# A hybrid decoder layer: a ninth column block on TensorE, the first norm on turned rows, sample dots in three parts

## The chip, the core and the metric

One core of a Trainium2 chip runs the whole layer as one program. The metric is device time in microseconds (us), from the start to the end of one execution; runs of one kernel are summed up by their median. Where the profile is used, its times belong to one profiled execution. PE is TensorE, PEld its weight loads, DVE VectorE, ACT ScalarE, POOL GpSimd, SP the engine that issues most DMAs.

## The reference

256 prompt tokens and 32 sample tokens (8 sequences of 4) of width 2048 pass one layer: a mixer (RWKV-7 heads beside sparse attention heads), an output projection, a norm, an expert mixer and a second norm. Cut to the part that the change touches:

```python
def layer_norm(x, g, b):
    mu = x.mean(-1, keepdims=True)
    var = jnp.mean(jnp.square(x - mu), -1, keepdims=True)
    return (x - mu) * lax.rsqrt(var + LN_EPS) * g + b

def peer_ffn(x, wq, subkeys, u_tab, v_tab):          # x: (tokens, 2048)
    q = (x @ wq).reshape(n, 8, 2, 128)               # 8 heads, two halves of a key
    s = jnp.einsum('nhcd,hckd->nhck', q, subkeys)    # 128 sub-keys for each half
    hv, hix = lax.top_k(s, 16)
    cand = (hv[:, :, 0, :, None] + hv[:, :, 1, None, :]).reshape(n, 8, 256)
    cand_e = (hix[:, :, 0, :, None] * 128 + hix[:, :, 1, None, :]).reshape(n, 8, 256)
    tv, tpos = lax.top_k(cand, 16)
    expert = jnp.take_along_axis(cand_e, tpos, axis=-1)      # 16 of 16384 experts a head
    gate = jax.nn.softmax(tv, axis=-1)
    h = gelu(einsum('cd,chkd->chk', x, u_tab[expert]))       # 128 dots of 2048 a token
    return einsum('chk,chkd->cd', gate * h, v_tab[expert])   # 128 rows added a token

x = layer_norm(ALPHA * x + concat(y_r, y_n) @ w_out, ln1_g, ln1_b)
x = layer_norm(ALPHA * x + peer_ffn(x, ...), ln2_g, ln2_b)
```

## The kernel before

The prompt's 256 tokens are two tiles of 128, t = 0 and 1, in the partitions. Work is written as Python generators that are woven together. A scheduler then orders the instructions of each engine by a simulated time and by priorities; `tc.issue_after` and `tc.keep_in_program_order` (called `pin`) tie some of them down. Each engine runs its instructions strictly in that order. Tiles live in pools that are stacked from the left or the right end of the on-chip memory; a pool that is closed gives its space to later ones, and a tile in such space waits for the last user of what lay there.

The stages from the output product on:

1. **out**: `out_part(8, YN)` multiplies the second half of the mixer's result by `w_out`. Each fp32 factor is split into a rounded high part and a low part, and three matmuls give the product. Beside it runs `sample_chain`, the layer for the 32 sample tokens up to their first expert product: 128 partitions hold 32 tokens x 4 groups, and each of 32 choices needs two **sample dots** (line 1548): POOL gathers a 128x1024 half row of `peer_u` (`gather`, line 450) into a ring of five `cw` tiles, and DVE multiplies and sums it.
2. **ln1**: `layer_norm` for each prompt tile: statistics, then ACT normalises, DVE multiplies by the scale g, DVE and POOL in turn add the shift b. PE turns the finished rows into `XT` (2048 features in partitions), from which high and low parts `XHq`, `XLq` are made. The rows go to `X1D` in HBM, and the first 1024 columns come back as `X1a`.
3. **wq**: the query product, 16 column blocks c of 128 columns (`pj`, line 1806), copied by ACT to `QP`. For each head `scores` multiplies by the sub-keys (ACT copies the result to a ring `TB`), and `choose` takes the best 16 on DVE (lines 1359 to 1404), with POOL adding candidate indices and masking them (`L1406`). `settle`, one head later, reduces the masked indices (line 1412) and writes them, doubled, to `GI` (line 1413), the gathers' index table.
4. **peer**: a prompt token needs 128 dots of 2048 columns. For the upper 1024 columns PE computes them for *all* 16384 experts: `dense(i1)`, 128 steps of 128 experts, loads a turned block `ur` of the table `peer_u_t` and multiplies its eight column blocks by the tokens: two blocks in plain fp32 (line 1841), six split into high and low parts (ACT casts `uh`, DVE subtracts `ul`, 18 matmuls, line 1848). For the lower 1024 columns the 256 **prompt dots** (2 tiles x 128 choices) are gathered rows again (line 1772, ring `rows` of five). Constants spread them: `NDW` a head in wq from the third head on (6 in all), `ND` plus an extra one every `8/NDN` dense steps (160 in all), and the rest in weigh.
5. **weigh**: 68 software-pipelined, pinned steps pick the dense scores of the chosen experts: step s builds one-hot tiles `oo` on DVE (line 1880), PE turns and multiplies them (lines 1884, 1892), DVE takes the products (`xj`, line 1903), ACT scales (`scaled`), PE puts the weights into a table `AW` (`put`, line 1922). The first 28 steps carry the remaining prompt dots, later ones the sample's v rows, summed into `fs`. Then the sample's second norm and its 16 stores follow (lines 1983 to 1990).
6. **V** and **fin**: 128 steps multiply the weights by the upper table `peer_v` (1536 columns) while DVE adds gathered rows for the other 512, then the last norm.

## Time and profile before

| what | us |
|---|---|
| runs shown | 2556.65, 2556.81, 2553.73 (median 2556.65) |
| profiled execution | 2551.85 |
| its span | 2549.9 |
| PE busy / DVE busy / POOL busy / ACT busy in the span | 2250.9 / 1901.8 / 1380.0 / 985.3 |
| last matmul of the output product starts | 1046.87 |
| first matmul of the query product | 1088.73 |
| first dense matmul | 1223.43 |
| first one-hot tile of weigh | 1662.19 |
| second table row of the V stage reaches PE | 1996.43 |

Times inside the execution count from the start of the span. A group of the profile names line, engine, operation and tiles, the shapes, the count, the busy time and the mean of one in ns, and then the idle time of that engine before such instructions, with what ended it. In the chain of waits each row is a piece of the path that ended last. A plain fp32 matmul of 128x256 stands in the records as two, a split one as one.

### The profile page before, as it was taken

How to read it: one execution, taken by the hardware profiler on the slowest of the kernel's cores; microseconds unless marked ns; L12 is line 12 of the kernel's file. 1: busy time of each engine (PE TensorE's matmuls, PEld its weight loads, DVE VectorE, ACT ScalarE, POOL GpSimd, SP SyncE). 2: the span in 40 equal slices, each digit the busy share in tenths (PEclk: the TensorE clock that was granted, in tenths of full speed). 3: DMA queues.
4: the chain of work that ended last, by engine and by line, in shares of the span. 5: the costliest groups of instructions: out<-in, count | busy, mean ns of one | idle time of the engine just before them, and what ended most of it. 6: DMA issues, size and time to landing. Idle time of an engine off the chain costs nothing.

```text
span 2549.9 us, 44379 instructions
## 1 busy us (share of the span) xinstructions
PE 2250.9 (88%) x16140; PEld 1870.8 (73%) x16140; DVE 1901.8 (75%) x4264; ACT 985.3 (39%) x1845; POOL 1380.0 (54%) x1393
## 2 busy tenths in 40 slices
...
GB/s 223 234 221 238 282 218 147 114 203 231 225 240 263 249 237 253 311 253 180 188 380 369 363 362 362 358 265 275 242 268 236 277 318 324 325 345 323 320 326 167
DMA packets 343227, 683.28 MB, mean 268 GB/s; under 512 B 82142, under 2 KB 200864, under 8 KB 341696
## 3 DMA queue, kind: packets, MB, share of 16 engines
...
## 4 chain that ended last, share of the span: by engine, by line
PE 59%; DVE 15%; DMA 12%; issue 6%; POOL 5%; ACT 1%; SPq 1%; DVEq 0%; POOLq 0%; ACTq 0%
PE pb L2040 20%; PE ph L1848 9%; PE pj L419 7%; DVE rows L1772 3%; DMA rows<-in_peer_u,gi 3%; PE ph L1841 2%; PE pa L1664 2%; PE pj L1806 2%; DMA co<-in_cache_cmp_kv,gidx 2%; PE p L1076 2%; DVE CA L473 1%; PE pa L1922 1%; PE ss L1492 1%; DMA big<-in_state_rwkv 1%; PE px L1892 1%
## 5 line engine op out<-in xcount | busy, mean ns | idle before, releaser
L450 POOL DMA_INDIRECT rows<-in_peer_u,gi x256 | 356.0, 1391 | 231.1 <-DVE rows L1772 181.0
L450 POOL DMA_INDIRECT rq<-in_peer_v,gi x256 | 375.3, 1466 | 172.3 <-DVE fP L2014 77.9
L1772 DVE SCALAR_TENSOR_TENSOR rows<-rows,x1a 128x1024 f32<-128x1024 f32 x256 | 309.6, 1234 | 14.8 <-DMA rows<-in_peer_u,gi 14.5
L419 PE MATMUL pj<-XH,wl 128*128 128x288 f32 (+1 forms) x752 | 231.5, 308 | 15.6 <-POOL wl L414 8.3
L1848 PE MATMUL ph<-XHd,uh 128*128 128x256 f32 x768 | 239.1, 311 | 4.1 <-ACT uh L1635 0.8
L419 PE MATMUL pj<-XH,wh 128*128 128x288 f32 (+1 forms) x752 | 229.1, 305 | 11.5 <-DVE ss L749 7.0
L1848 PE MATMUL ph<-XHd,ul 128*128 128x256 f32 x768 | 225.2, 294 | 15.4 <-DVE ul L1636 13.1
L419 PE MATMUL pj<-XL,wh 128*128 128x288 f32 (+1 forms) x752 | 225.7, 300 | 0.0
L1848 PE MATMUL ph<-XLd,uh 128*128 128x256 f32 x768 | 218.1, 284 | 0.0
L2040 PE MATMUL pb<-vl,ah 128*128 128x512 f32 x768 | 217.8, 392 | 0.3 <-DVE vl L2034 0.3
L2040 PE MATMUL pb<-vh,al 128*128 128x512 f32 x768 | 216.5, 390 | 0.0
L2040 PE MATMUL pb<-vh,ah 128*128 128x512 f32 x768 | 199.1, 395 | 17.3 <-ACT vh L2033 17.3
L412 ACT CAST wh<-wraw 128x512 fp32r<-128x512 f32 (+1 forms) x188 | 114.5, 616 | 226.7 <-PE pj L419 168.3
L1636 DVE TENSOR_TENSOR ul<-ur,uh 128x384 fp32r<-128x384 f32 x256 | 135.2, 559 | 88.0 <-ACT uh L1635 87.1
L2014 DVE SCALAR_TENSOR_TENSOR fP<-rq,ge,fP 128x512 f32<-128x512 f32 x254 | 189.8, 747 | 2.4
L2040 PEld LDWEIGHTS pb<-vh,ah 128*128 128x128 f32 x768 | 146.3, 191 | 48.9 <-ACT vh L2033 18.5
L473 DVE SCALAR_TENSOR_TENSOR CA<-co,wbc,CA 128x256 f32<-128x256 f32 x248 | 135.9, 585 | 51.6 <-DMA co<-in_cache_cmp_kv,gidx 51.5
L1635 ACT CAST uh<-ur 128x384 fp32r<-128x384 f32 x256 | 125.5, 515 | 111.9 <-PE ph L1848 54.3
L2040 PEld LDWEIGHTS pb<-vl,ah 128*128 128x128 f32 x768 | 145.5, 190 | 31.2 <-DVE vl L2034 0.7
L1848 PEld LDWEIGHTS ph<-XHd,ul 128*128 128x128 f32 x768 | 147.6, 193 | 27.1 <-DVE ul L1636 26.3
L2040 PEld LDWEIGHTS pb<-vh,al 128*128 128x128 f32 x768 | 145.0, 189 | 30.4
L419 PEld LDWEIGHTS pj<-XH,wl 128*128 128x128 f32 (+1 forms) x752 | 143.7, 191 | 27.4 <-DVE wl L414 10.9
...
## 6 DMA issues: line engine op xcount, KB each, us to landing
ur<-in_peer_u_t SPq DMA_DIRECT2D x128, 512.0 KB
...
wraw<-in_w_in SPq DMA_DIRECT2D x64, 128.0 KB
...
```

What stands on the lines that cost most here:

```text
L412: sc.copy(wh[:, :, :n], w[:, :, :n])
L419: last[2] = pe.matmul(pb[:n, :nt], wi[:, k, :n], xi[(o + k) // 8][:, (o + k) % 8, :nt], start=(o + k == 0 and wi is wh and xi is xh), stop ...
L450: gp.indirect_dma_start(out=dst, out_offset=None, in_=rows_, in_offset=bass.IndirectOffsetOnAxis(ap=ix, axis=0))
L473: ve.scalar_tensor_tensor(d_, x_, w_, d_, op0=OP.mult, op1=OP.add)
L1076: pe.matmul(pb[hs[c], 64 * m:64 * m + 64], lhs(hs[c], m), rhs(hs[c], m), start=True, stop=True)
L1635: sc.copy(xh, pb)
L1636: return ve.tensor_tensor(xl, pb, xh.bitcast(F32), OP.subtract)
L1664: pe.matmul(acc[t], xi[:, e, P * t:P * t + P], wi[:, e, :], start=(k == e == n_ == 0), stop=(k == 6 and e == 1 and n_ == 2))
L1772: i_ = ve.scalar_tensor_tensor(r_, r_, 1.0, X1a[t], op0=OP.mult, op1=OP.mult, accum_out=h_)
L1848: mm = pe.matmul(ph[:, :NPR], wi[:, e, :], xi[:, NSP // 2 * q + e, :], start=False, stop=(q == 1 and e == NSP // 2 - 1 and wi is wl))
L2014: ve.scalar_tensor_tensor(fP[t], r_, w_, fP[t], op0=OP.mult, op1=OP.add)
L2040: pe.matmul(acc[3 * t + q], wi[:, P * t:P * t + P], xi[:, 512 * q:512 * q + 512], start=(k == 0 and wi is ah and xi is vh), stop=(k == P - ...
```

## The change

- **Nine column blocks on PE.** `NDB` = 9: `peer_u_t` has 1152 columns a row (576 KB a step), and the dense step has a third plain fp32 matmul. The prompt dots shrink to `UG` = 896 columns, gathered from a new contiguous table `peer_u_g`. Indices are no longer doubled. `NDN` goes from 2 to 4 (192 dots in peer), and wq carries prompt dots only in its last two rounds.
- **First norm.** Statistics are taken as each block of the output product is finished. One inverse root serves both tiles. DVE normalises without scale and shift, PE turns these rows, and ACT applies scale and shift as per-partition factors while it writes `XT`. The row form gets scale (DVE) and shift (POOL) afterwards, is stored from POOL's queue, and 896 columns are loaded back in round h = 2. `XHd` (ACT) and `XLd` (POOL) are made from `XT`.
- **Sample dots in three parts.** 28 in out (`NSD` = 14 choices), 12 in ln1 behind the normalising (`NLD` = 6), 24 in wq, four a round, with a ring `sr` of five tiles and a second copy `sx4` of the sample's x.
- **Smaller moves.** `settle`'s index write goes to POOL; the first query weights load earlier; the pools of out, wq, peer and V are laid out in another order (the V stage's tiles `v_`, `vh` lie first); the second norm's tiles for the sample lie in `x1a`'s space and load at step 46; the last `scaled` calls alternate between ACT and DVE; `out_part` gets a priority of 400 in the weaving.

The core of the diff:

```diff
+NSD = 14
+NLD = 6
...
-NDN = 2
+NDN = 4
...
-NSP = 6
+NDB = 9
+SPLIT = ((0, 3), (3, 6))
+NSP = SPLIT[-1][1]
+UG = 128 * (16 - NDB)
...
-        gp.tensor_copy(HF, HI)
-        gp.tensor_scalar(HF[:, 0], HF[:, 0], 128.0, None, op0=OP.mult)
+        k_ = 2.0 if t == 2 else 1.0
+        for c in range(2):
+            gp.tensor_scalar(HF[:, c], HI[:, c], k_ if c else k_ * P, 0.0, op0=OP.mult, op1=OP.add)
...
-        EF = pool([P, 16], "EF")
+        EF = pool([P, 16], "EF", bufs=2)
         ve.tensor_reduce(EF, hit, AX.X, OP.add)
-        ve.tensor_scalar(GI[t][:, 16 * h:16 * h + 16], EF, 2.0, None, op0=OP.mult)
+        gp.tensor_copy(GI[t][:, 16 * h:16 * h + 16], EF)
...
-        hd = cx([P, 2, 32], "hd")
...
-        for s_ in range(32):
+        yield from sample_dots(ring, x4, 0, NSD)
+
+    def sample_dots(ring, x4, n0, n1):
+
+        for s_ in range(n0, n1):
...
+    def sample_formed():
...
+                    ve.bn_stats(out=lst[:, t, cq, :], in_=x_)
...
+    np_.close()
...
-    weave((chain, 32), (out_part(8, YN), 16))
+    weave((chain, NSD), (out_part(8, YN), 16, 400))
...
-    XH, XL = (xq([P, NSP, NPR], nm, F32R) for nm in ("XHq", "XLq"))
+
+    kw_ = Pool("kw", "right")
+    wring = lambda: kw_([P, 8, P], "wraw", bufs=WB)
+    def query_load(c, o):
+
+        w = wring()
+        sy.dma_start(w, w_q[:, 128 * c:128 * c + 128].rearrange("(k p) c -> p k c", p=P)[:, o:o + 8])
+        return w
+
+    wq_ = {(0, o): query_load(0, o) for o in (0, 8)}
...
-        layer_norm(lp, lambda c0, n: x1c(t, c0, n),
-                   *(lambda c0, n, nm=nm: gb1[nm, c0 // 1024][:, c0 % 1024:c0 % 1024 + n] for nm in ("ln1_g", "ln1_b")))
-        for hf in range(2):
-            sy.dma_start(X1D[P * t:P * t + P, 1024 * hf:1024 * hf + 1024], X1[t][hf])
+        ve.bn_aggr(out=lmv[:, t, :], in_=lst[:, t].rearrange("p a b -> p (a b)"))
+    ve.tensor_scalar(lv, lmv[:, :, 1], 1e-5, None, op0=OP.add)
+    rsqrt(lp, lrr, lv, "ln")
+    ve.scalar_tensor_tensor(lv, lmv[:, :, 0], -1.0, lrr, op0=OP.mult, op1=OP.mult)
+    for t in range(2):
         for q in range(4):
+            x_ = x1c(t, 512 * q, 512)
+            normed = ve.tensor_scalar(x_, x_, lrr[:, t:t + 1], lv[:, t:t + 1], op0=OP.mult, op1=OP.add)
...
-            tk = slice(P * t, P * t + P)
-            n4 = min(4, NSP - 4 * (q % 2))
-            k4, p4 = slice(4 * (q % 2), 4 * (q % 2) + n4), pb.rearrange("p (k t) -> p k t", k=4)
-            sc.copy(XT[:, 4 * q:4 * q + 4, tk], p4)
-            if q > 1:
-                columns(p4[:, :n4], XH[:, k4, tk], XL[:, k4, tk])
+            for e in range(4):
+                k = 4 * q + e
+                sc.activation(XT[:, k, P * t:P * t + P], pb[:, 128 * e:128 * e + 128], AF.Identity,
+                              bias=prm("ln1_b", 16, k), scale=prm("ln1_g", 16, k))
+    sq_ = Pool("sq", "right")
+    sx4 = sq_([P, D], "sx4")
+    for g in range(4):
+        sy.dma_start(sx4[32 * g:32 * g + 32, :], X1D[NPR:NT, :])
+    late = sample_dots(lambda: sq_([P, 1024], "sr", bufs=5), sx4, NSD, 32)
+    with tc.issue_after(normed.ins):
+        for _ in take(late, NLD):
+            pass
+        for hf in range(2):
+            for t in range(2):
+                for nm, op_ in (("ln1_g", OP.mult), ("ln1_b", OP.add)):
+                    for q in range(2):
+                        x_, y_ = (t_[:, 512 * q:512 * q + 512] for t_ in (X1[t][hf], gb1[nm, hf]))
+                        (ve if op_ is OP.mult else gp).tensor_tensor(x_, x_, y_, op_)
+                gp.dma_start(X1D[P * t:P * t + P, 1024 * hf:1024 * hf + 1024], X1[t][hf])
     oe.close()
+    cx[0].close()
     lp.close()
-    cx[0].close()
-    np_.close()
...
-    TB = up([P, 4, NPR], "TB")
-    X1a = [up([P, 1024], f"x1a{t}") for t in range(2)]
-    for t in range(2):
-        sy.dma_start(X1a[t], X1D[P * t:P * t + P, :1024])
...
-    kc, dp, kq = (Pool(nm, "left") for nm in ("kc", "dp", "kq"))
+    up([P, 1024], "rows", bufs=NRW)
+    xa_ = up([P, 2 * UG], "x1a")
+    X1a = [xa_[:, UG * t:UG * t + UG] for t in range(2)]
+    TB = up([P, 4, NPR], "TB")
+    dp, kc, kq = (Pool(nm, "left") for nm in ("dp", "kc", "kq"))
+    dp([P, NDB, P], "ur", bufs=NUR)
     XHd, XLd = dp([P, NSP, NPR], "XHd", F32R), dp([P, NSP, NPR], "XLd", F32R)
-    Xfd = dp([P, 8 - NSP, NPR], "Xfd")
+    Xfd = dp([P, NDB - NSP, NPR], "Xfd")
...
-            rows_[i] = up([P, 1024], "rows", bufs=NRW)
-            gather(rows_[i], uh2, GI[t][:, s_:s_ + 1])
+            rows_[i] = up([P, 1024], "rows", bufs=NRW)[:, :UG]
+            gather(rows_[i], a["peer_u_g"], GI[t][:, s_:s_ + 1])
...
-                    w = kw_([P, 8, P], "wraw", bufs=WB)
-                    sy.dma_start(w, w_q[:, 128 * c:128 * c + 128].rearrange("(k p) c -> p k c", p=P)[:, o:o + 8])
+                    w = wq_.pop((c, o), None) or query_load(c, o)
...
-                sc.copy(QP[:, c, :], pb[:, :NPR])
+                last_ = sc.copy(QP[:, c, :], pb[:, :NPR])
...
+        if h == 2:
+            for t in range(2):
+                sy.dma_start(X1a[t], X1D[P * t:P * t + P, :UG])
...
-                if h > 2:
+                for _ in take(late, 2):
+                    pass
+                if h > 6:
...
+    with tc.issue_after(chosen.ins), tc.issue_after(last_.ins):
+        for _ in late:
+            pass
+        sample_formed()
+    sq_.close()
     kw_.close()
-    sc.copy(XHd, XH)
-    sc.copy(XLd, XL)
-    sc.copy(Xfd, XT[:, 8 + NSP:, :])
+    for q in range(NSP // 2):
+        k2, x_ = slice(2 * q, 2 * q + 2), XT[:, 16 - NDB + 2 * q:18 - NDB + 2 * q, :]
+        sc.copy(XHd[:, k2, :], x_)
+        gp.tensor_tensor(XLd[:, k2, :], x_, XHd[:, k2, :].bitcast(F32), OP.subtract)
+    sc.copy(Xfd, XT[:, 16 - NDB + NSP:, :])
...
-        w = dp([P, 8, P], "ur", bufs=NUR)
+        w = dp([P, NDB, P], "ur", bufs=NUR)
...
-        for e in range(NSP, 8):
+        for e in range(NSP, NDB):
             pe.matmul(ph[:, :NPR], w[:, e, :], Xfd[:, e - NSP, :], start=(e == NSP), stop=False)
-        for q in range(2):
-            wh, wl = (dp([P, NSP // 2, P], nm, F32R, bufs=3) for nm in ("uh", "ul"))
+        for e0, e1 in SPLIT:
+            wh, wl = (dp([P, e1 - e0, P], nm, F32R, bufs=3) for nm in ("uh", "ul"))
             with tc.high_priority(offset=120 + 45 * i1 if i1 < NPRI else 0):
-                lo_ = columns(w[:, NSP // 2 * q:NSP // 2 * q + NSP // 2, :], wh, wl)
-            for e in range(NSP // 2):
+                lo_ = columns(w[:, e0:e1, :], wh, wl)
+            for e in range(e0, e1):
                 for wi, xi in ((wh, XHd), (wh, XLd), (wl, XHd)):
-                    mm = pe.matmul(ph[:, :NPR], wi[:, e, :], xi[:, NSP // 2 * q + e, :],
-                                   start=False, stop=(q == 1 and e == NSP // 2 - 1 and wi is wl))
+                    mm = pe.matmul(ph[:, :NPR], wi[:, e - e0, :], xi[:, e, :],
+                                   start=False, stop=(e == NSP - 1 and wi is wl))
...
-            o_ = hot[u][:, 0, e, :]
-            pin(sc.activation(o_, o_, AF.Copy, scale=TB[:, 2, 4 * u + e:4 * u + e + 1]))
+            o_, g_ = hot[u][:, 0, e, :], TB[:, 2, 4 * u + e:4 * u + e + 1]
+            if u < 60 or e % 2:
+                pin(sc.activation(o_, o_, AF.Copy, scale=g_))
+            else:
+                pin(ve.tensor_scalar(o_, o_, g_, None, op0=OP.mult))
...
+        if s_ == 46:
+            bs_, gs_, x_ = (xa_[:, 512 * n:512 * n + 512] for n in range(3))
+            for q in range(4):
+                r_, c_ = slice(32 * q, 32 * q + 32), slice(512 * q, 512 * q + 512)
+                sy.dma_start(x_[r_, :], X1D[NPR:NT, c_])
+                for t_, nm in ((gs_, "ln2_g"), (bs_, "ln2_b")):
+                    sy.dma_start(t_[r_, :], bass.AP(tensor=a[nm].tensor, offset=a[nm].offset + 512 * q, ap=[[0, 32], [1, 512]]))
...
+    vp([P, FD], "v_", bufs=2)
+    vp([P, FD], "vh", F32R, bufs=2)
     fP = [vp([P, 512], f"fP{t}") for t in range(2)]
+    vp([P, 512], "rq", bufs=NRQ)
...
-        u_[:, 1024:].reshape(P, P, 8, P).transpose(0, 3, 2, 1)).reshape(P * P, 1024)
+        u_[:, UG:].reshape(P, P, NDB, P).transpose(0, 3, 2, 1)).reshape(P * P, P * NDB)
+    arrays["in_peer_u_g"] = np.ascontiguousarray(u_[:, :UG])
...
```

The order of the instructions at three places. First DVE, from the end of the output product to the first choice. Before, with `cw` the gathered row of a sample dot, `x_00` to `x_11` the halves of the two prompt tiles, `wraw` the rows of scale and shift, `ln_t` and `lnrr` the inverse root (a piece, the first tile's):

```order
L1548 SCALAR_TENSOR_TENSOR cw,hd<-cw,x_10488 128x1024
L1630 TENSOR_TENSOR x_00_9703<-x_00_9703,wraw 128x512
L1631 TENSOR_TENSOR x_00_9703<-x_00_9703,wraw 128x512
L243 SCALAR_TENSOR_TENSOR lnrr<-ln_t,lnrr 128x1
L1630 TENSOR_TENSOR x_01_9704<-x_01_9704,wraw 128x512 x2
L1548 SCALAR_TENSOR_TENSOR cw,hd<-cw,x_10488 128x1024 x2
L241 TENSOR_TENSOR ln_t<-lnrr 128x1
L1631 TENSOR_TENSOR x_01_9704<-x_01_9704,wraw 128x512
L1548 SCALAR_TENSOR_TENSOR cw,hd<-cw,x_10488 128x1024 x2
```

The same place now, from the end of the one inverse root on (`lnv` holds the shift of the normalising, `sr` the row of a sample dot, `shT` its result; `HV<-TB` is the first choice):

```order
L248 SCALAR_TENSOR_TENSOR lnrr<-ln_t,lnrr 128x2
L1733 SCALAR_TENSOR_TENSOR lnv<-lnmv,lnrr 128x2
L1737 TENSOR_SCALAR x_00_9713<-x_00_9713,lnrr,lnv 128x512 x2
L1737 TENSOR_SCALAR x_01_9714<-x_01_9714,lnrr,lnv 128x512 x2
L1737 TENSOR_SCALAR x_10_9715<-x_10_9715,lnrr,lnv 128x512 x2
L1737 TENSOR_SCALAR x_11_9716<-x_11_9716,lnrr,lnv 128x512 x2
L1558 SCALAR_TENSOR_TENSOR sr,shT<-sr,sx_12077 128x1024 x5
L1758 TENSOR_TENSOR x_00_9713<-x_00_9713,wraw 128x512 x2
L1758 TENSOR_TENSOR x_01_9714<-x_01_9714,wraw 128x512 x2
L1758 TENSOR_TENSOR x_10_9715<-x_10_9715,wraw 128x512 x2
L1758 TENSOR_TENSOR x_11_9716<-x_11_9716,wraw 128x512 x2
L1558 SCALAR_TENSOR_TENSOR sr,shT<-sr,sx_12077 128x1024 x7
```

The eight normalising operations stand alone behind the root; twelve sample dots and eight multiplies follow them and stand ahead of the first choice.

Second POOL at the same place, now: additions of the shift (L1758), stores of the rows to `x1d` (L1759) and the gathers of sample rows (L456).

```order
L456 DMA sr<-in_peer_u,ig 128x1024
L1758 TENSOR_TENSOR x_00_9713<-x_00_9713,wraw 128x512 x2
L1758 TENSOR_TENSOR x_01_9714<-x_01_9714,wraw 128x512 x2
L1758 TENSOR_TENSOR x_10_9715<-x_10_9715,wraw 128x512
L1759 DMA x1d<-x_00_9713 128x1024
L1758 TENSOR_TENSOR x_10_9715<-x_10_9715,wraw 128x512
L1758 TENSOR_TENSOR x_11_9716<-x_11_9716,wraw 128x512 x2
L456 DMA sr<-in_peer_u,gi_72 128x1024
L1759 DMA x1d<-x_01_9714 128x1024
L456 DMA sr<-in_peer_u,ig 128x1024
```

Ten gathers lie ahead of the additions; those of the eleventh and twelfth of the twelve dots lie behind them.

Third DVE at the seam between two rounds of the choice, before (`hit` is the last line of one head's choice, `L1404`; `gi` the index table):

```order
L1404 TENSOR_TENSOR rows<-CT_61,TF 128x864 x2
L1412 TENSOR_REDUCE EF<-rows 128x16
L1413 TENSOR_SCALAR gi_70<-EF 128x16
L1412 TENSOR_REDUCE EF<-rows 128x16
L1413 TENSOR_SCALAR gi_71<-EF 128x16
L1772 SCALAR_TENSOR_TENSOR rows,hd_12208<-rows,x1a_12204 128x1024
L1359 MAX HV<-TB 128x8 x2
```

And now:

```order
L1410 CAST TF<-TI 128x16 x2
L1411 TENSOR_TENSOR rows<-CT_61,TF 128x864 x2
L1419 TENSOR_REDUCE EF<-rows 128x16 x2
L1558 SCALAR_TENSOR_TENSOR sr,shT<-sr,sx_12077 128x1024 x4
L1365 MAX HV<-TB 128x8 x4
```

Four sample dots stand where the two index writes and one prompt dot stood.

45 lines of the change are left out of this document (14 added, 31 removed).

## The prediction

> **What bounds the kernel now.** The page gives a span of 2549.9 us (profiled execution 2551.85; the median of the runs shown, 2556.65, is 4.8 more). I read the busy time by stage first, because a share of the whole span mixes stages with different limits. Columns: stretch and length; busy time of PE, PEld, DVE, ACT, POOL with instructions; granted clock; DMA share; GB/s.
>
> ```profile
> 967.00:1047.00 80.00, 61.80 (x232) 47.04 (x232) 70.78 (x101) 21.05 (x29) 57.48 (x39) 0.81 0.87 313
> 1048.00:1117.00 69.00, 22.92 (x96) 18.75 (x96) 55.64 (x110) 13.39 (x22) 39.89 (x31) 0.63 0.85 295
> 1117.00:1234.00 117.00, 113.18 (x558) 100.19 (x559) 100.53 (x481) 18.46 (x42) 64.58 (x118) 0.98 0.53 158
> 1234.00:1350.00 116.00, 103.64 (x684) 94.34 (x684) 96.99 (x221) 47.73 (x97) 65.74 (x63) 0.96 0.90 341
> 1350.00:1660.00 310.00, 303.30 (x2086) 276.26 (x2085) 231.65 (x433) 144.27 (x284) 173.02 (x120) 1.00 0.97 361
> 1662.00:1842.00 180.00, 106.48 (x540) 98.27 (x541) 172.26 (x464) 63.65 (x168) 127.28 (x90) 0.68 0.80 265
> 1842.00:1980.00 138.00, 133.11 (x1005) 96.77 (x1003) 90.73 (x381) 91.51 (x252) 68.42 (x60) 0.97 0.71 240
> ```
>
> The stages are: output product, first norm, query product with the choice of experts, dense score product (two rows), the first 28 weigh steps, and the rest of them. The limit changes hands. In the norm PE works a third of the time and waits for DVE. From 1117 to 1660 PE is nearly full. From 1662 to 1842 DVE is (172.26 of 180), and PE waits for it. After 1842 PE is full again. The change takes dots from DVE in the weigh stage and gives PE a longer dense stage, so these two prices decide, with what the norm releases.
>
> Two waits of PE show how the norm holds up the query product. The timeline of PE, idle time and releaser in brackets:
>
> ```profile
> 1046.87 0.39 PE L1664 MATMUL pa<-wl,YH 128*128 128x512 f32 x1
> ...
> 1088.73 14.76 PE L1806 MATMUL pj<-XT,wraw 128*128 128x256 f32 x64
> ...
> 1117.47 8.91 PE L1806 MATMUL pj<-XT,wraw 128*128 128x256 f32 x32 [13.98 <-ACT QP L1807]
> ...
> 1233.66 0.58 PE L1848 MATMUL ph<-XHd,ul 128*128 128x256 f32 x1 [3.33 <-DVE ul L1636]
> ```
>
> Call the end of the output product T0 (1047.3). The query product starts at T0+41. It stops again for 14 us, until the last sample dot is done and QP's space is free. Dense steps flow from 1233.7, T0+186, with about two of the 128 done before.
>
> **Part 1: output product and norm.** Five of the 33 sample dots before T0 leave that stretch.
>
> ```profile
> L1548 DVE SCALAR_TENSOR_TENSOR cw<-cw,x 128x1024 f32<-128x1024 f32 x33 | 48.3, 1478 | 8.7 <-DMA cw<-in_peer_u,ig 6.7 <-DMA cw<-in_peer_u,gi 1.9
> ```
>
> Five times 1.478 is 7.4 us, if DVE alone sets T0. It is busy 70.78 of that stretch's 80 us and PE 61.80, so DVE sets most of it: the gain lies between 0 and 7.4, and I take 5, T0 = 1042. Behind T0 the old norm shows the paces of DVE and POOL, and the chain of work those of a gathered row:
>
> ```profile
> 1050.24 0.24 DVE L1625 BATCH_NORM_AGGREGATE lnmv<-lnst 128x2 f32<-128x24 f32 x1
> ...
> 1054.98 0.15 DVE L1434 SCALAR_TENSOR_TENSOR lnmv<-lnmv,lnrr 128x1 f32<-128x1 f32 x1
> ...
> 1056.52 0.68 DVE L1630 TENSOR_TENSOR x<-x,wraw 128x512 f32<-128x512 f32 x1
> ...
> L1631 POOL TENSOR_TENSOR x<-x,wraw 128x512 f32<-128x512 f32 x4 | 6.1, 1534 | 0.7 <-DVE x L1630 0.6
> ...
> 1066.78 7.83 DMA cw<-in_peer_u,gi
> ```
>
> One tile's chain of small operations takes 4.9 us with two dots inside, some 3 without, and now serves both tiles. Eight normalising operations follow, 0.68 us each at most (5.5). Transposes and ACT operations come block by block; the last trails by about 3 us. So the query product starts at T0+12, and the 14 us stall goes: QP's space no longer waits for all the sample dots.
>
> PE cannot use all of this, because DVE's order puts twelve sample dots and eight multiplies ahead of the first choice, and POOL's order puts eight additions ahead of the gathers for the last two of these dots. The additions cannot start before DVE has done five dots and the first multiplies, about T0+16; they take 8x1.5 = 12 us. Then come a gather (1.4), its landing (7.8 on the chain) and the dots: the first choice begins at T0+42. Bounds: T0+35, when the third product block gives head 0's scores (12+3x6.9) and rows come sooner, and T0+46.
>
> **Part 2: choosing rounds.** Each head costs one round on DVE. Timelines of DVE, then POOL, in one round:
>
> ```profile
> 1188.38 0.48 DVE L1359 MAX8 HV<-TB 128x8 f32<-128x128 f32 x2
> ...
> 1197.70 1.04 DVE L1412 TENSOR_REDUCE EF<-rows 128x16 f32<-128x864 f32 x1
> 1198.66 1.92 DVE L1772 SCALAR_TENSOR_TENSOR rows<-rows,x1a 128x1024 f32<-128x1024 f32 x1
> ...
> 1200.51 1.83 DVE L1413 TENSOR_SCALAR gi<-EF 128x16 int32<-128x16 f32 x1
> ...
> 1203.53 0.17 DVE L1413 TENSOR_SCALAR gi<-EF 128x16 int32<-128x16 f32 x1
> 1203.62 0.48 DVE L1359 MAX8 HV<-TB 128x8 f32<-128x128 f32 x2
> ...
> 1196.88 5.43 POOL L1406 TENSOR_TENSOR rows<-rows,CE 128x864 f32<-128x864 f32 x2
> ```
>
> A round is 15.24 us: 9.3 of choosing (1188.38 to 1197.70) and 5.9 behind it. Now two reductions (2.1) and four sample dots stand there, and the index writes are on POOL. At the dots' 1.145 us start to start (part 4) four cost 4.6: 16.0 us, if POOL's multiplies disturb nothing. They do: the dot takes 1.92, and the index write 1.83 (0.17 at 1203.53, when POOL is idle), ending with POOL's pair at 1202.3. The most that the second multiply can add is its own 2.7: 18.7. I take 18.5, because dots stand beside it in every round. SBUF — State Buffer of the Trainium skill (section SBUF: two separate sides) says that a DVE operation with two SBUF inputs and a GpSimd operation that reads SBUF exclude each other for a whole instruction. The dot agrees with it; the index write has one input and was held all the same, which the sentence does not cover. By the rule a round is 18.7, 1 us more in the end; with ports truly shared it would be 16.0, and the time 15 us less.
>
> Round 0 has no reductions (16.6), rounds 1 to 5 are full, round 6 has one dot (12.5), and dense steps flow 3 us into round 7, as before: T0+42+16.6+5x18.5+12.5+3 = T0+167, about 1209, again with one or two done.
>
> **Part 3: dense product.** Nine column blocks, not eight, run on PE; the ninth is a third plain fp32 one beside the six split ones. The chain of work gives the price of such a matmul (64 records are 32 matmuls), the step, and two of the waits for rows:
>
> ```profile
> 1141.98 13.82 PE pj L1806 x64
> ...
> 1270.50 11.84 DMA rows<-in_peer_u,gi
> ...
> 1364.50 2.37 PE ph L1848 x18
> ...
> 1377.55 2.36 PE ph L1848 x18
> ```
>
> 13.82/32 = 0.432 us. Four steps take 13.05, so a step is 3.26, and becomes 3.69: **55 us more** on PE in all. Nothing hides this, as PE has 303.30 of 310 us busy. The others stay under it:
>
> ```profile
> L450 POOL DMA_INDIRECT rows<-in_peer_u,gi x120 | 174.1, 1451 | 138.8 <-DVE rows L1772 117.1 <-DVE ul L1636 15.3 <-issue 6.4
> L1772 DVE SCALAR_TENSOR_TENSOR rows<-rows,x1a 128x1024 f32<-128x1024 f32 x119 | 143.3, 1219 | 0.9 <-DMA rows<-in_peer_u,gi 0.9
> ```
>
> With 1.5 dots a step POOL needs 2.2 us; DVE's 231.65 of 310 is 2.4 a step and grows by a quarter dot, 0.3. DMA carries 576+1.5x448 = 1248 KiB a step, 346 GB/s, where 512+1.25x512 KiB in 3.26 us were 362. Before, 1233.7+126x3.26 = 1644.5 stood against a real end near 1661: 16 us were lost, mostly to rows while the DMA filled up (1234 to 1350). With less demand I take 12 (bounds 8 and 16). The dense product ends at 1209+126.5x3.69+12 = 1687, **26 us later**.
>
> **Part 4: weigh.** Dots left for it: before, 256-6-160 = 90; now 256-2-192 = 62, over 896 columns. DVE around one step (three dots):
>
> ```profile
> 1787.28 1.22 DVE L1880 TENSOR_TENSOR oo<-CT,TB 128x1024 f32<-128x1024 f32 x1
> ...
> 1789.83 1.22 DVE L1772 SCALAR_TENSOR_TENSOR rows<-rows,x1a 128x1024 f32<-128x1024 f32 x1
> ...
> 1790.97 1.22 DVE L1772 SCALAR_TENSOR_TENSOR rows<-rows,x1a 128x1024 f32<-128x1024 f32 x1
> ...
> 1793.27 1.22 DVE L1880 TENSOR_TENSOR oo<-CT,TB 128x1024 f32<-128x1024 f32 x1
> ```
>
> And from the groups of the whole span and of this stage:
>
> ```profile
> L2014 DVE SCALAR_TENSOR_TENSOR fP<-rq,ge,fP 128x512 f32<-128x512 f32 x254 | 189.8, 747 | 2.4
> ...
> L1884 PE MATMUL pt<-CT,oo 128*128 128x128 f32 x116 | 26.8, 374 | 68.1 <-DVE oo L1880 34.1 <-DVE TB L1911 34.0
> ```
>
> A step is 2.5 us of its own and dots at 1.145. The L2014 group, the same kind of operation over 512 columns, takes 0.747, which makes 0.92 ns a column: 896 columns save 0.12, leaving 1.03. 90x1.145-62x1.03 = 39 us; the mean step falls from 6.2 to 4.8. PE waits 68.1 us in 29 steps for DVE, 2.35 a step, so it needs about 3.8 and does not become the bound. Rows that land late may take a little: **38 us less** (bounds 30 and 40).
>
> **Part 5: tail.** The last scalings move half to DVE, and the sample's rows load earlier. But these lines stay in their order:
>
> ```profile
> 1982.48 6.03 SPq L1990 DMA_DIRECT2D out<-rows  x16
> ...
> 1988.56 0.37 SPq L1948 DMA_DIRECT2D v__20754<-in_peer_v  x1
> ...
> 1996.43 2.93 PE L2040 MATMUL pb<-vh,ah 128*128 128x512 f32 x6 [6.14 <-ACT vh L2033]
> ```
>
> The second table row still queues behind sixteen stores that wait for the sample's norm. I take 2 us less (0 to 4).
>
> **Edits put at nothing.** X's low parts for the dense product are now three POOL subtractions ahead of round 0's POOL work. DVE needs that work only in round 1, 17 us on; without this cover they cost three times POOL's 2.7. The norm's rows are stored from POOL's queue and read back by SP ahead of later query weights; the product feeds round 2 by then, 35 us on. The other placements move tiles for which the chain shows no wait: nothing, with 3 us either way in the range.
>
> **Sum:** +26-38-2 = -14 us against the profiled 2551.85: 2538; against the median, 2543.
>
> **Rivals.**
> - *Norm and rounds come out cheap* (T0 1040, choice from T0+35, rounds of 16 and 13.9 for the first, loss 8): dense flows from T0+144 = 1184 and ends at 1659, 2 us early; with 39 and 4 it is -45: 2512. For it: the index writes leave DVE, and PE stands ready 29 us sooner. Against it: POOL's pair in each round. Chance 0.20.
> - *The norm's gain is eaten*: T0 1046, rounds of 19.5, loss 14: dense flows from T0+173 and ends at 1700, +38, which 36 and 2 balance: 2557, no change. For it: PE, too, is busy to within a microsecond of T0. Chance 0.17.
> - *Slower: rounds of 22 us.* Four dots a round need rows that POOL gathers behind its own multiplies and only when a buffer is free, 5.8 us of issue and about 8 of landing. If DVE waits for them, dense flows from T0+188 = 1230 and, with a loss of 16, ends at 1713, +52; weigh and tail give 36: 2573. The break-even is 21 us a round. Against it: five buffers, and most of a round to refill them. Chance 0.19.
> - *Forecast*, 2543, its own range 2530 to 2553. Chance 0.44.
>
> **Numbers.** The range, 2513 to 2570, takes in all but the ends of the cheap and the slow case. Under 0.2% (5 us) cannot be told from no change. Faster 0.43+0.20 = 0.63; same 0.17 and the forecast's upper edge, 0.18; slower 0.19.
>
> **What would show it.** T0 near 1042; first query matmul at T0+12 without the 14 us stall; first choice at T0+42; rounds of 16 to 18.7 us; four dense steps in 14.8; dense end near 1687; 4.8 us between `oo` rows; the wait behind the stores still there. Rounds over 21, dense steps over 3.75 or weigh steps over 5.3 make it wrong.

## The result, and the profile after

The changed kernel takes **2523.18 us** (median of 4 runs, 2517.96 to 2526.88), the kernel before, run beside it, 2555.19 (4 runs): a ratio of 0.9864, 95% interval 0.9834 to 0.9894. So it is 32 us faster where 14 were forecast. The profiled execution is the slowest of the four, 2526.88 with a span of 2525.1, against 2549.9 before: 24.8 us less, and it is these 24.8 that the stages below share out; the other 7 cannot be placed in a stage. The same kernel was timed once more among the experiments, beside runs of before of its own: 2523.83, ratio 0.9844, interval 0.9814 to 0.9873.

The busy time by stage of the changed kernel (columns as before), with stretches set to its own stages: output product, norm and the first choice, choosing rounds, dense product in two parts, the first 28 weigh steps, the rest of them.

```profile
967.00:1053.00 86.00, 61.26 (x236) 46.91 (x234) 62.45 (x93) 21.92 (x31) 52.77 (x38) 0.80 0.86 293
1053.00:1100.00 47.00, 38.97 (x188) 34.31 (x188) 37.02 (x58) 12.65 (x36) 29.16 (x24) 0.93 0.75 247
1100.00:1223.00 123.00, 96.76 (x475) 85.29 (x475) 122.86 (x517) 15.31 (x40) 88.94 (x147) 0.92 0.69 214
1223.00:1350.00 127.00, 122.50 (x811) 112.22 (x812) 100.17 (x229) 49.72 (x105) 74.55 (x75) 0.98 0.92 346
1350.00:1686.00 336.00, 330.58 (x2209) 302.16 (x2207) 238.22 (x478) 131.57 (x277) 187.32 (x144) 1.00 0.97 356
1686.00:1820.00 134.00, 86.00 (x529) 79.03 (x528) 128.20 (x397) 60.14 (x161) 81.45 (x63) 0.81 0.72 219
1820.00:1956.00 136.00, 130.20 (x1022) 95.39 (x1021) 95.97 (x401) 92.52 (x252) 70.21 (x61) 1.00 0.73 244
```

In the rounds DVE is now full (122.86 of 123) and PE is not; the dense stretch is longer with PE as full as before; the weigh stretch is shorter and still DVE's.

The timeline of PE of the changed kernel, at the places that were forecast:

```profile
1052.07 0.39 PE L1667 MATMUL pa<-wl,YH 128*128 128x512 f32 x1
1058.21 6.02 PE L1740 MATMUL pa<-CT,x 128*128 128x128 f32 x32 [5.75 <-DVE x L1737]
1065.45 2.86 PE L1832 MATMUL pj<-XT,wraw 128*128 128x256 f32 x12 [1.23 <-ACT XT L1743]
...
1223.48 0.58 PE L1886 MATMUL ph<-XHd,ul 128*128 128x256 f32 x1 [22.41 <-DVE ul L1639]
```

The query product starts 13.0 us after T0 (41 before) and its 14 us stall is gone. This gain did not reach the dense product whole: PE stands idle for 22.41 us before the dense steps flow, waiting for a low part `ul` from DVE, which is in the rounds.

All stages in one table, in us. A is the start of the last transposes in front of the output product, T0 the end of that product, "flow" the matmul in the last row above (1233.66 before), the 28 steps run from the first to the 29th one-hot tile `oo`, V0 is the first matmul of the V stage. Each entry is a difference of two rows of the timeline.

| stage | before, us | after, us | difference | forecast |
|---|---|---|---|---|
| start to A | 985.9 | 987.0 | +1.0 | 0 |
| A to T0 (output product) | 61.3 | 65.5 | +4.2 | -5 |
| T0 to flow (norm, rounds) | 186.4 | 171.0 | -15.4 | -19.4 |
| flow to the first `oo` (dense) | 428.5 | 463.0 | +34.5 | +51 |
| 28 weigh steps | 176.5 | 134.0 | -42.5 | -38 |
| 29th `oo` to V0 | 145.3 | 138.3 | -7.0 | -2 |
| V0 to the end | 565.8 | 566.3 | +0.5 | 0 |

The dense stage came out 17 us better than forecast, weigh and tail 10 better, norm and output product 13 worse. The dense end stood at 1686.5, forecast 1687: a right number from two wrong ones (flow 14 late, dense 17 short).

### The profile page after: what moved, and what is told of

It is laid out like the page before. It is cut to its first block, busy times and chain, and to the rows that moved or that the text cites. A ratio compares the mean times of both kernels' runs of the same rounds, so it can differ in the third digit from the quotient of the medians.

```text
span 2525.1 us, 44824 instructions
## 1 busy us (share of the span) xinstructions
PE 2268.9 (90%) x16396; PEld 1889.5 (75%) x16396; DVE 1869.3 (74%) x4241; ACT 967.0 (38%) x1848; POOL 1367.5 (54%) x1422
## 3 DMA queue, kind: packets, MB, share of 16 engines
q1 hardware_dynamic: 245600, 350.97, 42.5%
## 4 chain that ended last, share of the span: by engine, by line
PE 34%; DVE 13%; issue 5%; DMA 3%; POOL 3%; ACT 2%; SPq 0%; DVEq 0%; POOLq 0%; ACTq 0%
PE pb L2085 20%; PE ph L1886 6%; POOL rows L456 2%; DVE rows L1802 2%; PE ph L1879 2%; DVE sr L1558 2%; PE px L1930 1%; PE pa L1963 1%; PE fs L1982 1%; DMA ur<-in_peer_u_t 1%; DVE oo L1918 1%; DVE ul L1639 1%; DVE xj L1941 1%; PE pt L1922 1%; DMA v__22882<-in_peer_v 1%
## 5 line engine op out<-in xcount | busy, mean ns | idle before, releaser
L456 POOL DMA_INDIRECT rq<-in_peer_v,gi x256 | 375.4, 1467 | 168.0 <-DVE fP L2059 73.0
L456 POOL DMA_INDIRECT rows<-in_peer_u_g,gi x256 | 329.9, 1289 | 242.5 <-DVE rows L1802 198.3
L1802 DVE SCALAR_TENSOR_TENSOR rows<-rows,x1a 128x896 f32<-128x896 f32 x256 | 272.4, 1092 | 3.8 <-DMA rows<-in_peer_u_g,gi 3.1
L418 ACT CAST wh<-wraw 128x512 fp32r<-128x512 f32 (+1 forms) x188 | 114.8, 616 | 223.8 <-PE pj L425 171.0
L1879 PE MATMUL ph<-Xfd,ur 128*128 128x256 f32 x768 | 187.6, 380 | 3.4 <-DMA ur<-in_peer_u_t 3.2
L2085 PEld LDWEIGHTS pb<-vh,ah 128*128 128x128 f32 x768 | 146.0, 191 | 47.8 <-ACT vh L2078 17.4
L1886 PEld LDWEIGHTS ph<-XHd,ul 128*128 128x128 f32 x768 | 146.5, 191 | 42.6 <-DVE ul L1639 42.5
L1888 ACT COPY AW<-ph 128x256 f32<-128x256 f32 x128 | 77.7, 607 | 225.8 <-PE ph L1886 198.0
```

The source lines that it names most:

```text
L418: sc.copy(wh[:, :, :n], w[:, :, :n])
L456: gp.indirect_dma_start(out=dst, out_offset=None, in_=rows_, in_offset=bass.IndirectOffsetOnAxis(ap=ix, axis=0))
L1802: i_ = ve.scalar_tensor_tensor(r_, r_, 1.0, X1a[t], op0=OP.mult, op1=OP.mult, accum_out=h_)
L1879: pe.matmul(ph[:, :NPR], w[:, e, :], Xfd[:, e - NSP, :], start=(e == NSP), stop=False)
L1886: mm = pe.matmul(ph[:, :NPR], wi[:, e - e0, :], xi[:, e, :], start=False, stop=(e == NSP - 1 and wi is wl))
L1888: return lo_, mm, sc.copy(AW[:, i1 // 64, :, i1 % 64], ph[:, :NPR])
```

## The experiments

In all of them the *changed* kernel is edited, in most at one place. Because A alone moves between 972 and 1000 us from one execution or chip to another, stages are compared rather than totals. The stretch from flow to the dense end, which these kernels are judged by, reads 461 to 467 us in the eight traces whose dense product is that of the changed kernel, and the 28 weigh steps 133.7 to 134.4.

### Blocks and dots: which of the two pays

Three kernels complete a square of eight or nine blocks with 1.25 or 1.5 dots a step.

```diff
 e1_eight_blocks
-NDB = 9
+NDB = 8
 e2_eight_fewer
-NDB = 9
+NDB = 8
-NDN = 4
+NDN = 2
 e3_nine_fewer
-NDN = 4
+NDN = 2
```

> The changed kernel with eight column blocks on TensorE instead of nine (dots over 1024 columns), its 1.5 dots a dense step kept. Theory (DMA is the floor under the dense step): a step then loads 512+1.5x512 = 1280 KiB; at the 356 to 371 GB/s that the dense stage reaches, that is 3.53 to 3.68 us, no shorter than the 3.62 of nine blocks; weigh's 62 dots cost 0.115 us more each, +7. Time about 2528 (2520 to 2536) against 2523. Rival (PE alone sets the step): the step is 3.26 as in the kernel before, dense is 45 us shorter, time near 2485.

> The changed kernel with eight column blocks and 1.25 dots a dense step, as in the kernel before; everything else of the change stays. Theory (the ninth block and its extra dots nearly pay for each other, and the gain of 25 to 32 us comes from the norm, the choice and the tail): dense step 3.26, dense ends 30 to 40 us earlier than the changed kernel's 1686, weigh's first 28 steps take about 177 us instead of 134; time about 2530 (2520 to 2540). Rival (the ninth block is what gives the gain): time 2545 or more.

> The changed kernel with its nine column blocks but only 1.25 dots a dense step, as before the change. Theory (the ninth block pays only because it lets the extra dots fit under the DMA): dense takes about 460 us from its flow on, as in the changed kernel (463), while 94 dots in weigh's first 28 steps take 2.48x28+94x1.03 = 166 us instead of 134; time about 2553 (2546 to 2562), slower than eight blocks with as many dots a step (2541). Rival (the ninth block brings the gain by itself): 2535 or less.

| kernel | blocks, dots a step | us | ratio to before (95%) | flow to dense end | 28 weigh steps | sum |
|---|---|---|---|---|---|---|
| e2_eight_fewer | 8, 1.25 | 2541.38 | 0.9938 (0.9912 to 0.9965) | 426.0 | 184.1 | 610.1 |
| e3_nine_fewer | 9, 1.25 | 2538.93 | 0.9968 (0.9938 to 0.9997) | 444.5 | 171.2 | 615.7 |
| e1_eight_blocks | 8, 1.5 | 2525.40 | 0.9860 (0.9828 to 0.9893) | 454.6 | 142.3 | 596.9 |
| changed | 9, 1.5 | 2523.18 | 0.9864 (0.9834 to 0.9894) | 463.2 | 134.0 | 597.2 |

e3 ran on a chip where the kernel before took 2546.52, so its ratio counts, not its time. e1 came out near 2528, as its theory said, and the next part shows that the theory was not the reason. e2 was a little slower than expected (2530), since weigh took 184.1 us and not 177; e3 is the slower of the two by ratio, as expected, with intervals that overlap, but its dense stage took 444.5 us where 460 were expected, and its weigh steps 171.2, not 166.

The ninth block costs the dense stage 18.5 us at 1.25 dots and 8.6 at 1.5, not the 55 of the forecast, and gives weigh 12.9 and 8.3. Beside a scatter of a few us **nothing is left of it**, and the ratios of e1 and the changed kernel agree. The quarter dot more in a dense step pays in both pairs, 13 and 18.5 us. Of the 32 us, some 16 are there with eight blocks and few dots (e2's ratio); by its stages they are in norm, rounds and tail.

### What holds the dense step

e1's number was the one expected from a floor set by the loads. The next kernel takes nearly all dots out of the dense stage, with eight blocks (one dot in four steps is left).

```diff
-NDB = 9
+NDB = 8
-NDN = 4
+NDN = 2
-ND = 1
+ND = 0
```

> The changed kernel with eight column blocks and one dot in four dense steps (1.25 before the change, 1.5 after it); the dots left go after the dense stage, which is long there. Theory (with eight blocks and 1.25 dots the dense step of 3.26 us waits for DMA; PE alone needs 3.02, as the first two steps of the kernel before show): with 512+0.25x512 = 640 KiB a step the steady step is 3.0 to 3.1 us. Rival (PE sets 3.26): the step stays at 3.2 or more. The time as a whole is much longer and says nothing.

Busy time of this kernel, by stretch:

```profile
1350.00:1600.00 250.00, 246.84 (x1787) 236.30 (x1786) 124.80 (x223) 125.22 (x243) 29.97 (x30) 1.00 0.70 231
```

Its copies of finished dense steps stand 12.06 us apart for every four, 3.015 a step; more than 80 in a row agree. The expectation of 3.0 to 3.1 for PE alone holds (the total, 2694.09, is long because these dots then stand in weigh). And PE is 99% busy in this stretch, hardly more than at 3.26 a step before (303.30 of 310, 98%): **busy time did not show the 0.24 us in each step that were not PE's own.**

That the loads take them is another matter, and the rows of single steps speak against it. In the steady part a step lasts one of a few fixed times, in a fixed sequence: before 3.02, 3.02, 3.78, 3.24; changed 3.45, 3.78, 3.78 in the first half and 3.45, 3.78 in the second; e1 3.02, 3.78, 3.78 and then 3.78, 3.23; e3, for 50 steps on end, 3.45. The long step is 3.78 with eight blocks and with nine. The timeline of the kernel before, PE and ACT in one step of 3.02 and one of 3.78 (rows of a single matmul and of other engines left out):

```profile
1605.63 1.03 PE L1841 MATMUL ph<-Xfd,ur 128*128 128x256 f32 x4
1605.83 0.63 ACT L1850 COPY AW<-ph 128x256 f32<-128x256 f32 x1 [0.69 <-PE ph L1848]
1606.31 0.47 PE L1848 MATMUL ph<-XHd,uh 128*128 128x256 f32 x1
...
1606.73 0.29 PE L1848 MATMUL ph<-XHd,ul 128*128 128x256 f32 x1
...
1608.65 1.03 PE L1841 MATMUL ph<-Xfd,ur 128*128 128x256 f32 x4
1608.85 0.60 ACT L1850 COPY AW<-ph 128x256 f32<-128x256 f32 x1 [2.39 <-PE ph L1848]
1609.26 0.93 ACT L1635 CAST uh<-ur 128x384 fp32r<-128x384 f32 x2
...
1609.83 0.39 PE L1848 MATMUL ph<-XHd,uh 128*128 128x256 f32 x1
...
1610.42 0.39 PE L1848 MATMUL ph<-XHd,ul 128*128 128x256 f32 x1
...
1612.43 0.81 PE L1841 MATMUL ph<-Xfd,ur 128*128 128x256 f32 x3
```

In the first step the first split matmul follows 0.68 us after the plain ones began. In the second it comes 1.18 after: ACT had done one `AW` copy, then sat 2.39 us in front of the next, which needs PE's finished step; only behind it stands the cast `uh` that PE's next step needs. PE gets `uh` 0.50 us late, and `ul`, which DVE makes from it, 0.67 (1.77 after the start; 1.10 in the free step). The step lasts 3.78, 0.76 more. The changed kernel, the same place:

```profile
1668.57 1.46 PE L1879 MATMUL ph<-Xfd,ur 128*128 128x256 f32 x6
1668.77 0.63 ACT L1888 COPY AW<-ph 128x256 f32<-128x256 f32 x1 [0.69 <-PE ph L1886]
1669.67 0.47 PE L1886 MATMUL ph<-XHd,uh 128*128 128x256 f32 x1
...
1672.01 1.46 PE L1879 MATMUL ph<-Xfd,ur 128*128 128x256 f32 x6
1672.21 0.60 ACT L1888 COPY AW<-ph 128x256 f32<-128x256 f32 x1 [2.82 <-PE ph L1886]
1672.62 1.38 ACT L1638 CAST uh<-ur 128x384 fp32r<-128x384 f32 x3
...
1673.19 0.40 PE L1886 MATMUL ph<-XHd,uh 128*128 128x256 f32 x1
1673.78 0.38 PE L1886 MATMUL ph<-XHd,ul 128*128 128x256 f32 x1
...
1675.80 1.46 PE L1879 MATMUL ph<-Xfd,ur 128*128 128x256 f32 x6
```

The copy, the cast and `ul` stand at the same distances, 0.20, 0.61 and 1.77 from the step's start, so the step lasts 3.78 again. But the third plain matmul covers 0.43 of the wait, and only 0.33 are left of 0.76. Over steps 20 to 124 the mean grew from 3.315 to 3.665, by 0.35 instead of 0.43, and over 126 steps that is some 10 of the missing 17 us. And e3:

```profile
1505.76 0.51 ACT L1638 CAST uh<-ur 128x384 fp32r<-128x384 f32 x1 [0.63 <-PE ph L1886]
...
1506.76 1.46 PE L1879 MATMUL ph<-Xfd,ur 128*128 128x256 f32 x6
1506.96 0.61 ACT L1888 COPY AW<-ph 128x256 f32<-128x256 f32 x1 [0.69 <-PE ph L1886]
1507.36 0.53 ACT L1638 CAST uh<-ur 128x384 fp32r<-128x384 f32 x1
...
1510.21 1.46 PE L1879 MATMUL ph<-Xfd,ur 128*128 128x256 f32 x6
...
1513.66 1.46 PE L1879 MATMUL ph<-Xfd,ur 128*128 128x256 f32 x6
```

Here the step's first cast is done before the copy (1505.76), the first split matmul follows the plain ones without a gap, and no step is held. What differs is written down in the programs, where ACT's instructions in the dense stage read, changed kernel first (its first half), then e3:

```
L1888 COPY AW<-ph 128x256
L1638 CAST uh<-ur 128x384 x4
L1888 COPY AW<-ph 128x256 x2
L1638 CAST uh<-ur 128x384 x2

L1888 COPY AW<-ph 128x256
L1638 CAST uh<-ur 128x384 x2
L1888 COPY AW<-ph 128x256
L1638 CAST uh<-ur 128x384 x2
```

Wherever two copies stand together, the casts of a step lie behind the copy of the one before it. Before, the pair came once in four steps; at 1.5 dots it comes once in two or three; in e11 and in e3's even part not at all.

The place of a step's first cast in ACT's order can be read for each step, and compared with the step's length (from the last split matmul of one step to that of the next, steps 20 to 124, 105 in each trace):

| kernel | casts behind the copy of the step before: steps, and their length | casts ahead of it: steps, and their length |
|---|---|---|
| before | 28, of them 23 at 3.78 | 77, of them 54 at 3.02 and 22 at 3.23 |
| e2_eight_fewer | 34, of them 31 at 3.78 | 71, of them 50 at 3.02 and 21 at 3.23 |
| e1_eight_blocks | 64, of them 58 at 3.78 | 41, of them 20 at 3.02 and 19 at 3.23 |
| e3_nine_fewer | 9, all at 3.78 | 96, of them 82 at 3.45 |
| changed | 63, of them 61 at 3.78 | 42, of them 40 at 3.45 |
| changed, repeated | 63, all at 3.78 | 42, of them 41 at 3.45 |

(Each length within 0.04 us.) So the place in ACT's order tells a step's length, within one kernel and its one stream of loads. The extra dot does not tell it: it comes every second step all along in the changed kernel, while at first two steps of three and then every second one are held. The order also accounts for most of what the quarter dot costs the dense stage: 54 more held steps at 0.33 are 18 of the 18.7 us with nine blocks, 30 at 0.76 are 23 of the 28.6 with eight. Why some free steps of eight blocks take 3.23 stays open.

Against the loads as the floor speaks also that the rate differs (GB/s by stretch: 363 before, 360 changed, 380 in e1, 337 in e3, each over 1350 to 1640), and that in 240 us of the changed kernel's dense stage ACT waits 10.6 us for the blocks `ur` but 114.3 for PE in front of the copies. So the theory behind e1's and e11's numbers fell while the numbers held. No run changed ACT's order alone: the link is read from the traces, where the order varies by itself, and e1, with a DMA share of 1.00, may sit near the loads' limit as well.

### Sample dots in the rounds

All 24 sample dots of the query stage are left out, with their gathers, so that a part of the sample's expert product is missing.

```diff
-                for _ in take(late, 2):
-                    pass
...
-        for _ in late:
-            pass
         sample_formed()
```

> The changed kernel without the 24 sample dots in the choosing rounds (left out altogether, so part of the sample's expert product is not computed). Theory (DVE paces the rounds and so the start of the dense product): rounds fall from 17.4 us to PE's pace of 14.7, dense flows from about 1203 instead of 1223.5, time about 2505. Rival (dense is bound by its loads from its start on, so that an earlier start only waits): dense ends at 1680 or later all the same, time 2517 or more.

2505.95 us, ratio 0.9789 (0.9761 to 0.9818), as expected. A steady round falls from 17.4 to 14.7 us. DVE of the changed kernel, in one round, then of this one:

```profile
1155.23 0.86 DVE L1365 MAX8 HV<-TB 128x8 f32<-128x128 f32 x4
...
1164.59 2.01 DVE L1419 TENSOR_REDUCE EF<-rows 128x16 f32<-128x864 f32 x2
1166.51 2.78 DVE L1558 SCALAR_TENSOR_TENSOR sr<-sr,sx 128x1024 f32<-128x1024 f32 x1
1169.22 1.22 DVE L1558 SCALAR_TENSOR_TENSOR sr<-sr,sx 128x1024 f32<-128x1024 f32 x1
...
1172.66 0.86 DVE L1365 MAX8 HV<-TB 128x8 f32<-128x128 f32 x4
```

```profile
1157.84 0.49 DVE L1365 MAX8 HV<-TB 128x8 f32<-128x128 f32 x2 [3.44 <-ACT TB L1385]
...
1172.55 0.49 DVE L1365 MAX8 HV<-TB 128x8 f32<-128x128 f32 x2 [3.44 <-ACT TB L1385]
```

The four dots take 6.15 us of a round (1166.51 to 1172.66). Without them DVE waits 3.44 for the scores in each round from the fourth on: the query product on PE is the next bound, 2.7 us lower.

### The first choice

Two kernels move work around it. e8 allows the dots to start behind the first replacement of a round, with a high priority; e14 has this, the later `sx` load of e10, and the additions of the row form on DVE instead of POOL.

```diff
 e8_dots_early
+            with tc.issue_after(mid[0].ins), tc.high_priority(offset=400):
+                for _ in take(late, 2):
+                    pass
 e14_dve_rows (besides)
-                        (ve if op_ is OP.mult else gp).tensor_tensor(x_, x_, y_, op_)
+                        ve.tensor_tensor(x_, x_, y_, op_)
```

> The changed kernel with the sample dots of a round put earlier on DVE, behind the first match-replace instead of behind the last comparison, where POOL's pair of multiplies runs. Theory (two of the four dots wait for POOL's multiplies, 2.9 us each instead of 1.2): rounds fall from 17.4 us to between 14.7 and 16, dense flows 8 to 14 us sooner after the first choice (now 123 us), time about 2514 (2508 to 2520). Rival (the waits only move to other two-input operations of DVE): rounds stay at 17 us or more, time 2520 or more.

> The changed kernel with three things altered: sample dots early in the rounds, the second copy of x loaded late, and the row form's eight additions on DVE beside its multiplies instead of on POOL. Theory (POOL's additions and DVE's multiplies and dots exclude each other: the eight multiplies take 13.2 us instead of 5): the first choice begins at 40 to 44 us behind the output product's end instead of 47.7, rounds take less as in the run with early dots, the time is 8 to 14 us under the changed kernel's beside it. Rival (DVE's own additions cost as much as the waits did): first choice at 47 or later, and no more than 5 us gained.

> The changed kernel once more, on the chip of the run before, for comparison. All theories: ratio 0.985 to 0.990 to the kernel before.

e8: 2511.32 us on the chip where before took 2546.52, ratio 0.9863 (0.9798 to 0.9928). The time is in the range expected, but not for the reason given: its rounds are uneven, 12.0 to 23.5 us, with dots of 2.1 to 2.8 us back in the second and third, and from the first choice to flow it saves 3 us, not 8 to 14. Beside e7 and e10 on the same chip (2521.54 and 2520.17) it is some 9 us faster, with intervals that overlap; no repeat of the changed kernel was run there. e14: 2525.07, ratio 0.9854 (0.9822 to 0.9885), beside the changed kernel's 2523.83 on the same chip (e15): no gain, where 8 to 14 us were expected. Yet its first choice starts 41 us after T0, not 47.7, and from T0 to the dense end its trace takes 625.6 us, against 633.9 in the changed kernel and 631.7 in the repeat: what a single trace gains here, six executions do not show in the total. The rows of ACT say what that choice waits for, in the changed kernel and then in e14:

```profile
1099.74 0.65 ACT L1385 COPY TB<-pb 128x256 f32<-128x256 f32 x2 [12.13 <-DMA x1d<-x]
```

```profile
1096.01 0.65 ACT L1388 COPY TB<-pb 128x256 f32<-128x256 f32 x2 [6.12 <-DMA x1d<-x]
```

The scores are there near 1088, but their copy waits for a *store*: the first norm's rows, which leave from POOL's queue behind the additions. All 13 traces of the changed kernel and its variants name this releaser, with 6 to 13 us; in three of them (e3, e7, e8) the landing of the third store is on record, and the copy starts 0.1 us behind it. That `TB` lies where the rows lay would explain it; no run placed it elsewhere.

### The output product

T0 came 4.2 us later after A where 5 less were forecast. Three kernels try a cause each: e4 holds the five early gathers of `sr` rows behind POOL's last `wl` of the stage, e5 drops the priority of 400, e10 loads the second copy of the sample's x behind the last load of `w_out` (`low_gp[0]` holds that `wl` in e4 and that load in e10). The repeat e15 measures the scatter.

```diff
 e4_hold_rows
-    with tc.issue_after(normed.ins):
+    with tc.issue_after(normed.ins), tc.issue_after(low_gp[0].ins):
         for _ in take(late, NLD):
 e5_no_priority
-    weave((chain, NSD), (out_part(8, YN), 16, 400))
+    weave((chain, NSD), (out_part(8, YN), 16))
 e10_sx_late
-    for g in range(4):
-        sy.dma_start(sx4[32 * g:32 * g + 32, :], X1D[NPR:NT, :])
+    with tc.issue_after(low_gp[0].ins):
+        for g in range(4):
+            sy.dma_start(sx4[32 * g:32 * g + 32, :], X1D[NPR:NT, :])
```

> The changed kernel with the gathers of the norm's first five sample rows held on POOL behind the output product's last subtraction there (they now stand amid its own gathers). Theory (these early rows take POOL and DMA time from the output product's sample rows, and DVE, in order, makes the product's low parts late): the output product ends at 1047 or earlier instead of 1053, dense flows about 5 us sooner, time about 2518. Rival (something else in the output stage, such as the pools' new places or the priority, made it late): its end stays at 1053 and the time is 2523 or a little more, as the rows land later.

> The changed kernel without the priority of 400 for the output product in the weaving. Theory (the priority puts the product's sums and statistics before the low parts of the weights on DVE, which makes the stretch from the last turn of the attention's output to the end of the output product 64 to 65 us instead of 61): 62 us or less. Rival: 63 us or more, and what lengthened the stretch stays open.

> The changed kernel with the second copy of the sample's x loaded behind the last load of the output weights, instead of at the start of that stretch. Theory (this 1 MB load, and not the five early rows, delays the sample rows there, and DVE, in order, the product's low parts): from the last turn of the attention's output to the end of the output product 62 us or less instead of 65.5 (61.3 in the kernel before), time about 2520. Rival (neither; the product is late for the order of its own work on DVE): 64 us or more, time as the changed kernel's.

A to T0: before 61.3; changed 65.5, repeated 63.5; e4 64.6 (2533.41 us, ratio 0.9886, 0.9846 to 0.9925); e5 64.7 (a single run, 2525.48); e10 62.8 (2520.17 us, ratio 0.9891, 0.9837 to 0.9945). Neither the held gathers nor the priority brings the stage back. e10 is lowest, but 0.7 from the repeat, where the same kernel differs by 2.0 between two executions. In all 13 traces with the change the stretch takes 62.8 to 65.5 us. PE's longest wait in this stage of the changed kernel, and the idle times of DVE from 987 to 1053 by what ended them, in all, times and longest:

```profile
1002.37 0.79 PE L1667 MATMUL pa<-wl,YH 128*128 128x512 f32 x1 [6.49 <-DVE wl L1662]
```

```profile
DVE wl L1662 <- ACT wh L1661: 8.5, 3, 5.4
DVE cw L1558 <- issue: 4.3, 1, 4.3
DVE cw L1558 <- DMA cw<-in_peer_u,ig: 2.7, 1, 2.7
```

Between A and T0 DVE is busy 49.3 us, 59.3 before, and idle some 16, 2 before. The 4.3 and 2.7 stand in front of two sample dots, and only behind these dots DVE makes the `wl` for which PE waits 6.49. Eleven of the 13 traces show this, with 4.5 to 7.1 us of idle time in front of such dots (1.0 before); in e10 and e14 PE's longest wait is for a `wl` of POOL. So DVE still stands in front of T0, but with waiting and not with work, and fewer dots brought nothing. Why these rows come later than before is not settled.

### The split of the last scalings

All `scaled` calls go back to ACT.

```diff
-if u < 60 or e % 2:
+if u < 64 or e % 2:
```

> The changed kernel with all scalings on ACT again; the sample's rows still load at step 46. Theory (the last puts are paced by ACT's four scalings a step): from step 28 to the first matmul of the V stage 141 us or more instead of 138.3, time about 2526. Rival (the earlier loads of the sample's rows alone made this stretch shorter): 138 to 139 us and no change of the time.

2521.54 us on the chip of 2546.52, ratio 0.9888 (0.9836 to 0.9940). The 29th `oo` to V0 takes 138.8 us, against 138.3, as the rival of this expectation has it: the split is not where most of the tail's 7 us come from. Behind the sample's last sum it takes 18.3 us instead of 17.2, so by these two traces some 1 us is the split's.

## Why the prediction was right, and where not

- **Direction and mechanism: right, the size too small.** Dots leave weigh, the norm's stall goes, the dense product grows, and the gain exceeds the price. Norm, dense product, weigh and tail all moved in the forecast direction. Yet 2523 lies below the forecast's own range (2530 to 2553), though inside the stated one.
- **Dense product: the step that failed.** "A step is 3.26, and becomes 3.69: 55 us more on PE in all. Nothing hides this, as PE has 303.30 of 310 us busy." The price of the matmul was right: the even step is 3.02 with eight blocks and 3.45 with nine, 0.43 more. But 3.26 was a mean of held and free steps, and the matmul hid partly in the held ones. The mean rose by 0.35 (in the second half, four steps of the changed kernel take 14.47 us, 13.06 before), the stage by 34.5. The further "16 us were lost, mostly to rows", of which 12 were forecast to stay, became about 7.
- **Weigh: right, a little small.** 4.8 us were forecast for the mean step, 134.0/28 is 4.79. Over the 28 steps DVE's busy time fell by 40.7 us (168.9 to 128.2), its idle time by 1.8 (7.6 to 5.8): it is the dots, as forecast. A step of two dots at 896 columns, DVE of the changed kernel:

```profile
1709.88 1.22 DVE L1918 TENSOR_TENSOR oo<-CT,TB 128x1024 f32<-128x1024 f32 x1
...
1712.31 1.09 DVE L1802 SCALAR_TENSOR_TENSOR rows<-rows,x1a 128x896 f32<-128x896 f32 x1
...
1713.32 1.09 DVE L1802 SCALAR_TENSOR_TENSOR rows<-rows,x1a 128x896 f32<-128x896 f32 x1
...
1714.34 1.22 DVE L1918 TENSOR_TENSOR oo<-CT,TB 128x1024 f32<-128x1024 f32 x1
```

  1.01 start to start, forecast 1.03, and 4.46 the step.
- **Rounds: mechanism right, sizes near.** The first two take 18.9 and 18.8, the next four 17.4, where 16.6 and then 18.5 were forecast; from the first choice to flow it is 123.3 us, forecast 125. In a steady round one of the four dots stands beside POOL's multiplies and takes 2.78. The forecast weighed 18.7 by SBUF — State Buffer of the Trainium skill (section SBUF: two separate sides), where a DVE operation with two SBUF inputs and a GpSimd operation that reads SBUF exclude each other, against 16.0 with shared ports. The held dot agrees with the rule. The same sentence of that page also names DVE operations in a 2-port mode, which the forecast left out when it said that the held index write was not covered; no trace tells the mode of that write. The price is less than 18.7 since most of POOL's pair (8.6 to 13.0 us of the round) now lies beside the two reductions (9.4 to 11.4), which have one input and run at 1.0 each.
- **First choice: late, for a reason not seen.** Forecast T0+42 within 35 to 46, measured T0+47.7. The forecast followed DVE's order and POOL's gathers, and DVE was done with the last of the twelve dots at T0+43.6, near it. The rest is a wait that was in none of its steps, that of the scores' own tile for a store in POOL's queue:

```profile
1100.14 0.87 DVE L1365 MAX8 HV<-TB 128x8 f32<-128x128 f32 x4 [4.13 <-ACT TB L1385]
```

  The eight multiplies, too, took 13.22 us and not the 5 that eight at 0.6 make. Seven of them took 0.68 to 0.72; one began at 1070.69, just ahead of POOL's additions, and ended at 1079.61, behind the sixth of them:

```profile
1066.99 13.22 DVE L1758 TENSOR_TENSOR x<-x,wraw 128x512 f32<-128x512 f32 x8
1071.01 6.17 POOL L1758 TENSOR_TENSOR x<-x,wraw 128x512 f32<-128x512 f32 x5
```

  In e14, with the additions on DVE, all sixteen operations take 0.68 to 0.72.
- **Output product: wrong in sign** (-5, measured +2 to +4). "It is busy 70.78 of that stretch's 80 us" was read as DVE's work setting T0; with 10 us less to do, DVE only waited more, some of it with PE waiting behind it.
- **Tail: mis-sized** (-2, measured -7). 2.8 of it lie behind the last sum of the sample, whose norm now loads its data sooner; the other 4 are in steps 29 to 64. That the earlier load is the cause of the first part, and what that of the second is, was not tested. The wait behind sixteen stores stayed as forecast:

```profile
1970.56 1.79 PE L2085 MATMUL pb<-vh,ah 128*128 128x512 f32 x4 [4.93 <-ACT vh L2078]
```

The rivals: the measured time lies between the forecast's range and the cheap rival's 2512, but that rival's conditions did not come (T0 1040 and T0+35, measured 1052 and T0+47.7), and its dense end, 1659, was 27 us early. "The norm's gain is eaten" had the flow at T0+173 (measured T0+171), by rounds of 19.5 that did not come, and missed the dense stage; "slower" named rounds of 22 us, and they took 17.4.
